# A hybrid attention and SwiGLU layer on one core: loads reordered at the start, partial output tiles begun early, one weight block of the down projection loaded later

## The chip, the cores and the metric

One core of one Trainium2 chip. The metric is device time in microseconds of one execution of the whole kernel; 665.92 us is the median of three runs before the change (665.73 to 667.33).

## What is computed

One decoder layer on x of 512 tokens by 1024 features, float32, then a final RMSNorm:

```
xn = rms_norm(h, norm1_g)
aq, ak, av, bq, kc, vc, ksl, vsl, kw, vw, gl = split_columns(xn @ w_in)
o_a = mixer_dilated(aq, ak, av)                    # 8 heads, three dilation patterns
o_b = g0 * o_cmp + g1 * o_slc + g2 * o_win         # 8 heads: compressed, selected, window
h = h + concat(o_a, o_b) @ w_out
hn = rms_norm(h, norm2_g)
h = h + (silu(hn @ w_gate) * (hn @ w_up)) @ w_down # hidden width 2816
out = rms_norm(h, norm_f_g)
```

The bias tables of attention come from a small table `rel_bias` by relative distance.

## The kernel before, in words

Every matrix product is made in three parts: an operand is split into a high part (a cast to float32r) and a low part (operand minus high), and TensorE adds high x high, high x low and low x high in one PSUM bank (`mm3`, lines 86 to 90). For a weight tile, `split` (line 77) loads it into one of three `w_raw` buffers on SP's queue (line 80), and writes high and low into one of five `w_hl` buffers, by ScalarE, VectorE or GpSimd as the table `ENG` says (lines 70, 72, 83).

**Order of work.** Most of the kernel is laid out as a program in order, and a planner (the tile framework) assigns each instruction its place on its engine from a timeline that it simulates, earlier program text first where several are ready; it also hands out the buffers. Where the source says `tc.manual_schedule(...)`, the named engines keep the order of the source. `tc.issue_after(x)` puts the instructions of its block behind x on x's engine alone. Each engine works in its own order and waits for what an instruction needs; SP's queue issues the transfers, one after the other, and waits in the same way.

**Start (lines 99 to 204).** SP issues `g_sb` (the norm gains, line 106), `rel_sb` and `oh_sb` (lines 144, 147), then x and the first weights. Twelve 128 x 128 products of ones (line 153) keep TensorE busy, four small products (line 157) build the bias rows. `load(kt)` (line 175) brings one of eight row blocks of x (line 177), scales and splits it on ScalarE and VectorE (lines 178, 179), and `project_0` makes the first projections. ScalarE loads its function table when its first function, the scaling of x, comes.

**Attention (lines 300 to 569).** Projections, bias tables, scores, softmax, transposes and the products with v, for 16 heads in the order of `PLAN`. `out_a` (line 481) makes half of the output projection for each of eight feature tiles and stores it, with x added, as `hp` in DRAM. The last head ends in `finish_head` and `finish_pair` (lines 360 to 371), which write the last of eight mixed tiles, high part on ScalarE (line 70), low part on GpSimd (line 371).

**Passage (lines 572 to 780).** The buffers of pool `ff` lie where those of attention were, so the first transfer into them waits for attention's last reader. `out_b(f)` (line 641) loads `hp` (line 643), makes the other half of the output projection over the mixed tiles 4 to 7 in one of four PSUM banks (two `proj`, two `S`), and VectorE adds (line 650). From it `lower` and `upper` (lines 614, 627) make the operands X1 and X2 of the feed-forward products, and `turn` (line 607) transposes the tile for the second norm. The products of gate and up are made by a scheme with seven products for eight (Strassen's, in Winograd's form), with sums of weights and of operands made on VectorE. `weights(j)` (line 691) is a generator that loads, adds and splits the weights of unit j in two parts; `first_part` and `second_part` (lines 718 to 747) are the unit's products.

```
    for f in range(KT - DELAY, KT):
        turn(f)
    w0.update(next(ahead))
    units = {0: first_part(0, w0)}
    with tc.issue_after(done):
        units[1] = first_part(1)
```

**Down projection (lines 785 to 1000).** Again seven products for eight, each over eleven row blocks in six steps (`PAIRS`). B11, B21, B22 and B12 are the four blocks of `w_down`, eleven loads of 256 KB each. SP keeps a written order (line 818): B11, B21, the residual `h1d` (line 832), B22, B12, then the final gain row `gf` (line 839). In a product's step, `prepare` splits both operands, and then the side work of that product runs: sums of operands on VectorE (`s1` to `s4`), weights added into B11 by accumulating transfers on GpSimd's queue (`add_w`, line 859), and `t3`, which adds B22 to B12 on VectorE. VectorE, ScalarE, GpSimd and TensorE keep the order of the source here. In the table, a product has its banks, its two operands, whether it starts the banks, its side work, what is evicted after it, and which output tiles are then closed. `close` squares a finished tile on ScalarE and multiplies its left half by `gf` on VectorE (`gain`), in the fourth step of the following product.

Of the kernel before, what the change touches and what calls it, by code (L numbers as in the profile page):

```python
# [11 lines left out]
F32 = mybir.dt.float32  # L12
F32R = mybir.dt.float32r
AF = mybir.ActivationFunctionType
ALU = mybir.AluOpType
# [36 lines left out]
def tile_hybrid_layer(ctx: ExitStack, tc: tile.TileContext, xT, w_qk0, w_t, w_av, w_vb, w_o, w_gu, w_d,  # L52
# [10 lines left out]
    def bank(tag):  # L63
        return psum.tile([P, 512], F32, name=tag, bufs=BANKS[tag])
# [9 lines left out]
    def tt(e, out, in0, in1, op):  # L74
        engines[e].tensor_tensor(out=out, in0=in0, in1=in1, op=op)  # L75

    def split(src, n, hi, lo):

        raw = ws.tile([P, WC], F32, name="w_raw", bufs=BUFS["w_raw"])
        nc.sync.dma_start(raw[:, :n], src)  # L80
        w = ws.tile([P, 2, WC], F32R, name="w_hl", bufs=BUFS["w_hl"])
        copy(hi, w[:, 0, :n], raw[:, :n])
        engines[lo].tensor_tensor(out=w[:, 1, :n], in0=raw[:, :n], in1=w[:, 0, :n].bitcast(F32), op=ALU.subtract)  # L83
        return w

    def mm3(ps, w, sl, xh, xl, first, last, skip=False):

        nc.tensor.matmul(ps, w[:, 0, sl], xh, start=first, stop=False, skip_group_check=skip)  # L88
        nc.tensor.matmul(ps, w[:, 0, sl], xl, start=False, stop=False, skip_group_check=skip)  # L89
        nc.tensor.matmul(ps, w[:, 1, sl], xh, start=False, stop=last, skip_group_check=skip)  # L90
# [12 lines left out]
    ii = const.tile([P, 64], F32, name="ii")  # L103
    nc.vector.tensor_tensor(out=ii, in0=ident[:, 0:64], in1=ident[:, 64:128], op=ALU.add)
    g_sb = const.tile([P, 2, KT], F32, name="g_sb")
    nc.sync.dma_start(g_sb, gT.rearrange("p (a k) -> p a k", a=2))
    cb_sb = const.tile([P, 2], F32, name="cb_sb")
    cw2_sb = const.tile([P, 3, DH], F32, name="cw2_sb")
    pos_sb = const.tile([P, 2, CSTRIDE], F32, name="pos_sb")
# [31 lines left out]


    rel_sb = const.tile([33, 16], F32, name="rel_sb")
    nc.sync.dma_start(rel_sb[0:32], rel)
    nc.vector.memset(rel_sb[32:33], 1.0)
    oh_sb = at.tile([33, 2, TW], F32, name="PTh")
    nc.sync.dma_start(oh_sb, oh.rearrange("b (a v) -> b a v", a=2))
    gd = dram.tile([16, RB, TW], F32, name="gd")
    gs = at.tile([16, 2, TW], F32, name="PTl")
    g1 = dram.tile([16, TW], F32, name="gh")  # L150
    warm = bank("S")
    for _ in range(12):
        nc.tensor.matmul(warm[:, :P], ones, ones, start=True, stop=True)
    for a in range(2):
        for c in range(2):
# [325 lines left out]
    def out_a(f, tok):  # L481

        w = split(w_o[f, :, 0:512], 512, *ENG[tok][:2])
        ps = bank("proj")
        for ft in range(4):
            mm3(ps, w, slice(ft * P, (ft + 1) * P), mixh[ft], mixl[ft], ft == 0, ft == 3)
        xr = at.tile([P, S], F32, name="pf", bufs=BUFS["pf"])
        nc.sync.dma_start(xr, xT[f * P:(f + 1) * P, :])
        if MISC["oa"] == "v":
            nc.vector.tensor_tensor(out=xr, in0=ps, in1=xr, op=ALU.add)  # L490
        else:
            y = at.tile([P, S], F32, name="pf", bufs=BUFS["pf"])
            nc.scalar.copy(y, ps)
            tt(MISC["oa"], xr, xr, y, ALU.add)
        nc.sync.dma_start(hp[f * P:(f + 1) * P, :], xr)
# [45 lines left out]
    for step in PLAN.split():  # L541
        n, i = step[0], step[1:]
        if n == "A":
            mix_a(int(i[0]), int(i[1]))
        elif n == "B":
            mix_b(int(i[0]), int(i[1]), i[2] == "w")
        elif n == "C":
            made["cmp", int(i)] = cmp_probs(made["b", int(i)], int(i), made["mlp"][0])
        elif n == "q":
            made["q", int(i)] = make_q(proj_t(2 * int(i) - 2, step), "Qa", e=MISC["tq"])  # L550
        elif n == "k":
            made["k", int(i)] = make_k(proj_t(2 * int(i) - 1, step), "a", 0, e=MISC["tk"])
        elif n == "b":
            made["b", int(i)] = make_q(proj_t(10 + int(i), step), "Qb", 2, MISC["tb"])
        elif n == "s":
            made["ksl"] = make_k(proj_t(8, step), "b", 1, 2, MISC["ts"])
        elif n == "w":
            made["kw"] = make_k(proj_t(9, step), "b", 2, 2, MISC["tw"])
        elif n == "v":
            project_vb((2 * int(i), 2 * int(i) + 1), step)  # L560
        elif n == "r":
            made["r" + i] = blocks(6 + int(i), int(i), step)
        elif n == "c":
            made["c" + i] = compress(made["r" + i], int(i), step)
        elif n == "m":
            made["mlp"] = compress_mlp((made["c0"], made["c1"]))
        elif n == "o":
            out_a(int(i), step)
    ph1.close()


# [8 lines left out]
    def split2(raw, hi, lo, w=None):  # L580

        if w is None:
            w = ff.tile([P, 2, 2, WC], F32R, name="hl2", bufs=BUFS["hl2"])
        copy(hi, w[:, 0], raw)
        tt(lo, w[:, 1], raw, w[:, 0].bitcast(F32), ALU.subtract)
        return w
# [40 lines left out]
    def upper(k, e):  # L627
# [10 lines left out]
        copy("a", X2[0][:, k, 2:5], f)  # L638
        tt("v", X2[1][:, k, 2:5], f, X2[0][:, k, 2:5].bitcast(F32), ALU.subtract)

    def out_b(f):
        xr = ff.tile([P, S], F32, name="g", bufs=BUFS["g"])
        nc.sync.dma_start(xr, hp[f * P:(f + 1) * P, :])
        w = split(w_o[f, :, 512:1024], 512, *ENG["ob"])
        ps = bank(("proj", "S")[f % 2])
        for ft in range(4, KT):
            mm3(ps, w, slice((ft - 4) * P, (ft - 3) * P), mixh[ft], mixl[ft], ft == 4, ft == KT - 1)
        h1 = ff.tile([P, S], F32, name="h1", bufs=BUFS["h1"])
        h1s[f] = h1
        nc.vector.tensor_tensor(out=h1, in0=ps, in1=xr, op=ALU.add)  # L650

    ss = ff.tile([P, NT, 2], F32, name="ss", bufs=1)

# [37 lines left out]
    def weights(j):  # L691

        l0 = raw2()
        nc.sync.dma_start(l0[:, 0], w_gu[j, 0, :, 0:WC])
        if j == 0:
            cd = raw2()
            c, d = cd[:, 0], cd[:, 1]
        else:
            c, d = raw1(), raw1()
        nc.sync.dma_start(c, w_gu[j, 1, :, 0:WC])  # L700
        nc.sync.dma_start(d, w_gu[j, 1, :, WC:])
        tt("v", l0[:, 1], c, d, ALU.add)
        w0 = split2(l0, "a", "v")
        yield {"a": w0[:, :, 0], "S1": w0[:, :, 1]}
        l1, l2 = raw2(), raw2()
        nc.sync.dma_start(l1[:, 1], w_gu[j, 0, :, WC:])
        tt("v", l1[:, 0], l0[:, 1], l0[:, 0], ALU.add)
        w1 = split2(l1, "a", "v")
        tt("v", l2[:, 0], l1[:, 0], l1[:, 1], ALU.add)
        tt("v", l2[:, 1], c, l0[:, 0], ALU.add)  # L710
        yield {"S2": w1[:, :, 0], "b": w1[:, :, 1], "S4": split1(l2[:, 0], "a", "v"), "S3": split1(l2[:, 1], "a", "v"),
               "d": split1(d, "a", "v")}

    def product(ps, w, X, b, first):
# [44 lines left out]
    for f in range(KT):  # L759
# [8 lines left out]
        if f == 2:  # L768
            ahead = weights(0)
            w0 = next(ahead)  # L770
    for f in range(KT - DELAY, KT):
        turn(f)
    w0.update(next(ahead))
    units = {0: first_part(0, w0)}
    with tc.issue_after(done):
        units[1] = first_part(1)
    second_norm()
# [45 lines left out]
    with tc.manual_schedule(engines={mybir.EngineType.SP}):  # L823
        r11 = [raw2() for _ in PAIRS]
        B11 = r11[:5] + [r11[5][:, 0:1]]
        load_w(B11, 0, 0)
        x0 = [ff.tile([P, n, WC], F32, name=tag, bufs=1)
              for n, tag in ((4, "X10"), (4, "X11"), (10, "X20"), (10, "X21"))]
        B21 = [x0[k // 2][:, 2 * (k % 2):2 * (k % 2) + 2] for k in range(4)] + [x0[2][:, 8:10], r11[5][:, 1:2]]
        load_w(B21, 1, 0)  # L830
        for t in range(NT):
            nc.sync.dma_start(x0[2][:, 2 * t:2 * t + 2], h1d[t].rearrange("p (c n) -> p c n", c=2))
        B22 = [x0[3][:, 2 * k:2 * k + 2] for k in range(5)] + [raw1()[:, None]]
        load_w(B22, 1, 1)
        B12 = [ws.tile([P, 2, WC], F32, name="w_hl", bufs=BUFS["w_hl"]) for _ in range(5)] + [raw1()[:, None]]
        load_w(B12, 0, 1)
        gf = [ff.tile([P, HD], F32, name="g", bufs=BUFS["g"]) for _ in range(2)]
        for c in range(2):
            nc.sync.dma_start(gf[c], gf_row[:, c * HD:(c + 1) * HD].to_broadcast([P, HD]))
# [22 lines left out]
    def t2(k):  # L862
        if k < 4:
            add_w(1, 1)(k)
        else:
            tt("v", B11[k], B11[k], B22[k], ALU.add)

    def t3(k):
        tt("v", B12[k], B12[k], B22[k], ALU.add)

    def evict(ps, th, c, sign=1):

# [21 lines left out]
    def store(t):  # L894
# [7 lines left out]
        (ps_a, A11, B11, True, (s3, add_w(0, 1)), [(ps_a, 0, 0)], []),  # L902
        (ps_b, A12, B21, True, (s1,), [(ps_b, 0, 0)], [(0, 0), (1, 0)]),
        (ps_c, A21, B11, True, (s2, t2), [(ps_c, 1, 1)], []),
        (ps_a, A21, B11, False, (s4, add_w(1, 0)), [(ps_a, 0, 1, -1)], []),
        (ps_c, A12, B22, False, (t3,), [(ps_c, 0, 1)], [(0, 1), (1, 1)]),
        (ps_a, A11, B12, False, (), [(ps_a, 1, 1, -1), (ps_a, 1, 0)], [(2, 1), (3, 1)]),
        (ps_b, A22, B11, True, (), [], [])]
    steps = [(n, k) for n in range(7) for k in range(len(PAIRS))]

# [152 lines left out]
```

## Time and profile before

| | |
|---|---|
| median of three runs | 665.92 us (665.73 to 667.33) |
| the profiled execution | 669.47 us, of which span 667.6 us |
| TensorE busy | 628.0 us, 94% of the span, 3876 products |
| VectorE busy | 530.5 us, 79% |
| ScalarE busy | 379.5 us, 57% |
| GpSimd busy | 170.0 us, 25% |
| DMA | 92.29 MB, mean 138 GB/s |

The profile is of one execution; its times run from the span's start. PE is TensorE, PEld its weight loads, DVE VectorE, ACT ScalarE, POOL GpSimd, SP SyncE; a q behind a name is that engine's queue of transfers and waits. A product's duration holds the time in the pipe, so products overlap; in the chain of work that ended last, a piece lasts from its start to the next one's. In a row of the timeline the brackets give how long the engine stood idle before the instruction and what ended that. Tile names carry no buffer numbers.

### The profile page before, as it was taken

How to read it: one execution, taken by the hardware profiler on the slowest of the kernel's cores; microseconds unless marked ns; L12 is line 12 of the kernel's file. 1: busy time of each engine (PE TensorE's matmuls, PEld its weight loads, DVE VectorE, ACT ScalarE, POOL GpSimd, SP SyncE). 2: the span in 40 equal slices, each digit the busy share in tenths (PEclk: the TensorE clock that was granted, in tenths of full speed). 3: DMA queues.
4: the chain of work that ended last, by engine and by line, in shares of the span. 5: the costliest groups of instructions: out<-in, count | busy, mean ns of one | idle time of the engine just before them, and what ended most of it. 6: DMA issues, size and time to landing. Idle time of an engine off the chain costs nothing.

```text
span 667.6 us, 11272 instructions
## 1 busy us (share of the span) xinstructions
PE 628.0 (94%) x3876; PEld 560.3 (84%) x3876; DVE 530.5 (79%) x1072; ACT 379.5 (57%) x785; POOL 170.0 (25%) x214
## 2 busy tenths in 40 slices
PE   9999997989999999987899999999999999859995
PEld 6878887868878888767799999999999988748784
DVE  4558867567787768649899989989999779669995
ACT  4553566245684668747864555555555636615572
POOL 6635852063445555430000000000000040414000
PEclk9999999979999999989899999999999999969998
DMA  5766576346415651043543333233233499949011
GB/s 178 211 189 188 168 182 165 100 132 164 130 36 172 187 192 33 1 163 106 189 141 102 108 127 122 87 111 109 97 113 108 164 258 322 305 85 160 1 63 63
DMA packets 52803, 92.29 MB, mean 138 GB/s; under 512 B 7643, under 2 KB 10971, under 8 KB 52748
## 3 DMA queue, kind: packets, MB, share of 16 engines
q1 hardware_dynamic: 47852, 82.68, 39.3%
q0 software_dynamic: 4320, 7.87, 6.8%
q10 hardware_dynamic: 576, 1.05, 0.4%
q8 instruction: 30, 0.49, 0.3%
q14 instruction: 25, 0.20, 0.1%
HBM read 76.32 MB, written 7.64 MB: 126 GB/s over the span
## 4 chain that ended last, share of the span: by engine, by line
PE 70%; DMA 11%; DVE 9%; ACT 5%; issue 3%; SPq 1%; POOL 1%; ACTq 0%; DVEq 0%; POOLq 0%
PE proj L88 8%; PE proj L90 8%; PE proj L89 8%; PE S L88 6%; PE S L89 6%; PE S L90 6%; PE PT L339 3%; DMA g<-in_gf_dram 2%; DMA X<-h1d 2%; PE S L316 2%; PE O L355 2%; PE O L358 2%; PE S L317 2%; DMA w_raw<-in_w_t_dram 1%; DMA X<-in_w_d_dram 1%
## 5 line engine op out<-in xcount | busy, mean ns | idle before, releaser
L859 POOL DMA_DIRECT2D raw<-in_w_d_dram x30 | 26.5, 1041 | 287.8 <-DVE hl L75 280.8
L70 ACT CAST hl<-raw 128x1024 fp32r<-128x1024 f32 (+1 forms) x69 | 70.5, 1022 | 40.5 <-PE S L930 16.7
L75 DVE TENSOR_TENSOR hl<-raw,hl 128x1024 fp32r<-128x1024 f32 (+1 forms) x69 | 81.2, 1178 | 3.0 <-ACT hl L70 2.9
L70 ACT CAST w_hl<-w_raw 128x512 fp32r<-128x512 f32 (+2 forms) x76 | 43.3, 576 | 63.6 <-PE S L90 19.2
L83 POOL TENSOR_TENSOR w_hl<-w_raw,w_hl 128x512 fp32r<-128x512 f32 (+1 forms) x47 | 61.2, 1306 | 65.2 <-ACT w_hl L70 26.2
L336 POOL TENSOR_SCALAR P<-P,den 128x512 f32<-128x512 f32 (+1 forms) x96 | 51.1, 551 | 39.9 <-DVE den L328 28.1
L324 ACT ACTIVATE P<-P,mn 128x512 f32<-128x512 f32 (+1 forms) x96 | 53.5, 558 | 11.8 <-DVE mn L322 11.5
L75 DVE TENSOR_TENSOR PTl<-PT,PTh 128x512 fp32r<-128x512 f32 (+2 forms) x96 | 43.8, 482 | 10.2 <-ACT PTh L349 9.7
L349 ACT CAST PTh<-PT 128x512 fp32r<-128x512 f32 (+2 forms) x96 | 38.1, 426 | 22.7 <-PE PT L339 18.8
L88 PE MATMUL S<-X,w_hl 128*128 128x256 f32 x176 | 49.9, 284 | 1.0 <-DVE h1t L75 0.5
L88 PE MATMUL S<-X,hl 128*128 128x256 f32 x176 | 50.0, 284 | 0.7 <-ACT xf L724 0.7
L322 DVE CUSTOM_DVE_ANT_0 P<-S,T 128x512 f32<-128x512 f32 (+1 forms) x96 | 43.9, 483 | 8.2 <-PE S L317 6.7
L89 PE MATMUL S<-X,hl 128*128 128x256 f32 x176 | 50.0, 284 | 0.3 <-DVE X L75 0.3
L89 PE MATMUL S<-X,w_hl 128*128 128x256 f32 x176 | 49.8, 283 | 0.0
L90 PE MATMUL S<-X,hl 128*128 128x256 f32 x176 | 49.7, 282 | 0.0
L90 PE MATMUL S<-X,w_hl 128*128 128x256 f32 x176 | 49.6, 283 | 0.0
L88 PE MATMUL proj<-xh,w_hl 128*128 128x512 f32 x112 | 46.1, 412 | 1.2 <-DVE va L281 1.1
L70 ACT CAST w_hl<-raw 128x512 fp32r<-128x512 f32 x45 | 27.3, 620 | 32.3 <-PE S L90 25.7
L90 PE MATMUL proj<-xh,w_hl 128*128 128x512 f32 x112 | 45.6, 407 | 0.0
L89 PE MATMUL proj<-xl,w_hl 128*128 128x512 f32 x112 | 45.4, 406 | 0.0
L83 DVE TENSOR_TENSOR w_hl<-w_raw,w_hl 128x512 fp32r<-128x512 f32 (+1 forms) x37 | 26.1, 710 | 15.0 <-ACT w_hl L70 14.9
L339 PE MATMUL PT<-ident,P 128*128 128x128 f32 x240 | 36.1, 273 | 0.8 <-POOL P L336 0.8
(305 smaller groups left out, 2047.5 us busy)
## 6 DMA issues: line engine op xcount, KB each, us to landing
raw<-in_w_gu_dram SPq DMA_DIRECT2D x46, 256.0 KB, 3.3
w_raw<-in_w_gu_dram SPq DMA_DIRECT2D x42, 256.0 KB, 2.7
raw<-in_w_d_dram POOLq DMA_DIRECT2D x30, 256.0 KB, 8.1
w_raw<-in_w_t_dram SPq DMA_DIRECT2D x28, 256.0 KB, 3.1
X<-in_w_d_dram SPq DMA_DIRECT2D x20, 256.0 KB, 7.5
T<-gd SPq DMA_DIRECT2D x64, 64.0 KB, 2.0
w_raw<-in_w_o_dram SPq DMA_DIRECT2D x16, 256.0 KB, 3.0
raw<-in_w_d_dram SPq DMA_DIRECT2D x12, 256.0 KB, 3.8
```

Of the source, the lines that this page charges most:

```text
L70: nc.scalar.copy(out, in_)
L75: engines[e].tensor_tensor(out=out, in0=in0, in1=in1, op=op)
L83: engines[lo].tensor_tensor(out=w[:, 1, :n], in0=raw[:, :n], in1=w[:, 0, :n].bitcast(F32), op=ALU.subtract)
L88: nc.tensor.matmul(ps, w[:, 0, sl], xh, start=first, stop=False, skip_group_check=skip)
L89: nc.tensor.matmul(ps, w[:, 0, sl], xl, start=False, stop=False, skip_group_check=skip)
L90: nc.tensor.matmul(ps, w[:, 1, sl], xh, start=False, stop=last, skip_group_check=skip)
L322: nc.vector.tensor_tensor_reduce(out=pp, in0=sv, in1=T[:, S - w:], op0=ALU.add, op1=ALU.min, scale=1.0, scalar=3e38, accum_out=mn[:, t:t + 1])
L324: nc.scalar.activation(pp, pp, AF.Exp, bias=mn[:, t:t + 1], scale=-1.0, accum_out=den[:, t:t + 1])
L336: nc.gpsimd.tensor_scalar(pp, pp, den[:, t:t + 1], 1.0, op0=ALU.mult, op1=ALU.mult)
L339: nc.tensor.transpose(pv[:, kb * P:(kb + 1) * P], pp[:, kb * P:(kb + 1) * P], ident)
L349: nc.scalar.copy(ov[0], pv)
L859: nc.gpsimd.dma_start(B11[k][:, i], rows_w(kh, ch, k, i), accum_op=ALU.add)
```

## The change

Start: x is the first transfer on SP; `g_sb`, `rel_sb` and `oh_sb` go to ScalarE's queue, ScalarE runs one small Square before, and nine products of ones take the place of twelve. Passage: `out_b` is cut in two; `out_b_start` makes the nine products over the mixed tiles 4 to 6, for tiles 0 to 3 ahead of the rest, and for tile 4, in a `PT` bank, behind the last TensorE instruction of the last head. The first products of unit 0 come before the last three turns, and `weights` yields its second part in two. Down projection: B12 has no buffers of its own; `load_12` loads it on GpSimd's queue into B21's, in the fourth product, `t3` and the sixth product use it there, and the accumulation `add_w(1, 0)` moves from the fourth to the fifth product.

```diff
-    nc.sync.dma_start(g_sb, gT.rearrange("p (a k) -> p a k", a=2))
+    nc.scalar.dma_start(g_sb, gT.rearrange("p (a k) -> p a k", a=2))
...
-    nc.sync.dma_start(rel_sb[0:32], rel)
+    nc.scalar.dma_start(rel_sb[0:32], rel)
...
-    nc.sync.dma_start(oh_sb, oh.rearrange("b (a v) -> b a v", a=2))
+    nc.scalar.dma_start(oh_sb, oh.rearrange("b (a v) -> b a v", a=2))
...
+    nc.scalar.activation(nt[:, 0:1], ones[:, 0:1], AF.Square)
     warm = bank("S")
-    for _ in range(12):
+    for _ in range(9):
...
+    head_end = [i for i in nc.cur_bb.bb.instructions[-60:] if i.engine == mybir.EngineType.PE][-1]
     ph1.close()
...
+    started = {}
+
+    def out_b_start(f):
+
+        w = split(w_o[f, :, 512:1024], 512, *ENG["ob"])
+        ps = bank("PT" if f == 4 else ("proj", "S")[f % 2])
+        for ft in range(4, KT - 1):
+            mm3(ps, w, slice((ft - 4) * P, (ft - 3) * P), mixh[ft], mixl[ft], ft == 4, False)
+        started[f] = w, ps
+
     def out_b(f):
+        if f not in started:
+            out_b_start(f)
+        w, ps = started.pop(f)
         xr = ff.tile([P, S], F32, name="g", bufs=BUFS["g"])
         nc.sync.dma_start(xr, hp[f * P:(f + 1) * P, :])
-        w = split(w_o[f, :, 512:1024], 512, *ENG["ob"])
-        ps = bank(("proj", "S")[f % 2])
-        for ft in range(4, KT):
-            mm3(ps, w, slice((ft - 4) * P, (ft - 3) * P), mixh[ft], mixl[ft], ft == 4, ft == KT - 1)
+        ft = KT - 1
+        mm3(ps, w, slice((ft - 4) * P, (ft - 3) * P), mixh[ft], mixl[ft], False, True)
...
+    for f in range(4):
+        out_b_start(f)
+    with tc.issue_after(head_end):
+        out_b_start(4)
...
         w1 = split2(l1, "a", "v")
+        yield {"S2": w1[:, :, 0], "b": w1[:, :, 1]}
         tt("v", l2[:, 0], l1[:, 0], l1[:, 1], ALU.add)
         tt("v", l2[:, 1], c, l0[:, 0], ALU.add)
-        yield {"S2": w1[:, :, 0], "b": w1[:, :, 1], "S4": split1(l2[:, 0], "a", "v"), "S3": split1(l2[:, 1], "a", "v"),
+        yield {"S4": split1(l2[:, 0], "a", "v"), "S3": split1(l2[:, 1], "a", "v"),
                "d": split1(d, "a", "v")}
...
-    for f in range(KT - DELAY, KT):
-        turn(f)
+    units = {0: first_part(0, w0)}
+    early = [i for i in nc.cur_bb.bb.instructions[-40:] if i.engine == mybir.EngineType.PE][-1]
+    with tc.issue_after(early):
+        for f in range(KT - DELAY, KT):
+            turn(f)
     w0.update(next(ahead))
-    units = {0: first_part(0, w0)}
+    w0.update(next(ahead))
...
-        B12 = [ws.tile([P, 2, WC], F32, name="w_hl", bufs=BUFS["w_hl"]) for _ in range(5)] + [raw1()[:, None]]
-        load_w(B12, 0, 1)
...
+    def load_12(k):
+        for i in range(B21[k].shape[1]):
+            nc.gpsimd.dma_start(B21[k][:, i], rows_w(0, 1, k, i))
+
     def t3(k):
-        tt("v", B12[k], B12[k], B22[k], ALU.add)
+        tt("v", B21[k], B21[k], B22[k], ALU.add)
...
-        (ps_a, A21, B11, False, (s4, add_w(1, 0)), [(ps_a, 0, 1, -1)], []),
-        (ps_c, A12, B22, False, (t3,), [(ps_c, 0, 1)], [(0, 1), (1, 1)]),
-        (ps_a, A11, B12, False, (), [(ps_a, 1, 1, -1), (ps_a, 1, 0)], [(2, 1), (3, 1)]),
+        (ps_a, A21, B11, False, (s4, load_12), [(ps_a, 0, 1, -1)], []),
+        (ps_c, A12, B22, False, (t3, add_w(1, 0)), [(ps_c, 0, 1)], [(0, 1), (1, 1)]),
+        (ps_a, A11, B21, False, (), [(ps_a, 1, 1, -1), (ps_a, 1, 0)], [(2, 1), (3, 1)]),
```

## Rows read from the trace of the kernel before

**Rows 1.** Stretches of 20 us: busy us (instructions) by engine, clock, DMA, GB/s.
```profile
core 0: us, PE busy (x) PEld busy (x) DVE busy (x) ACT busy (x) POOL busy (x), PEclk, DMA share, GB/s
300.00:320.00 20.00, 15.03 (x89) 13.06 (x87) 20.00 (x38) 16.07 (x33) 0.00 (x0) 0.91 0.41 151
...
580.00:600.00 20.00, 9.96 (x33) 7.66 (x33) 10.80 (x16) 4.61 (x7) 1.92 (x3) 0.74 0.52 117
600.00:620.00 20.00, 20.00 (x90) 16.57 (x89) 19.76 (x26) 11.43 (x17) 7.91 (x9) 1.00 0.85 142
```

**Rows 2.** Waits of PE and of DVE, 535 to 600: us in total, times, longest.
```profile
PE S L929 <- DVE hl L75: 10.0, 1, 10.0
...
DVE X L75 <- DMA g<-in_gf_dram: 10.5, 1, 10.5
```

**Rows 3.** Timeline of SP's queue, 505 to 660: start, us, issue.
```profile
566.51 6.43 SPq L813 DMA_DIRECT2D w_hl<-in_w_d_dram  x10
...
573.94 1.20 SPq L839 DMA_DIRECT2D g<-in_gf_dram  x2
```

**Rows 4.** Chain that ended last, 530 to 667: start, us, what.
```profile
573.94 14.81 DMA g<-in_gf_dram
...
593.08 0.43 PE S L930
...
597.35 0.43 PE S L928
...
598.04 0.23 PE S L930
...
629.47 0.50 PE PT L929
```

**Rows 5.** Stretch of 3 us inside DVE's wait, columns as in rows 1.
```profile
585.00:588.00 3.00, 0.00 (x0) 0.00 (x0) 0.00 (x0) 0.00 (x0) 0.00 (x0) 0.92 1.12 261
```

**Rows 6.** Timeline of DVE: end of its wait, first `t3`, one split.
```profile
589.20 1.29 DVE L75 TENSOR_TENSOR X<-X,g 128x512 f32<-128x512 f32 x2 [10.48 <-DMA g<-in_gf_dram]
...
612.11 1.22 DVE L75 TENSOR_TENSOR w_hl<-w_hl,X 128x1024 f32<-128x1024 f32 x1
...
628.20 1.21 DVE L75 TENSOR_TENSOR hl<-w_hl,hl 128x1024 fp32r<-128x1024 f32 x1
```

**Rows 7.** Timeline of POOL's queue: two pairs of accumulating loads, third product.
```profile
574.91 1.76 POOL L859 DMA_DIRECT2D raw<-in_w_d_dram  x2 [0.73 <-DVE hl L75]
578.42 1.75 POOL L859 DMA_DIRECT2D raw<-in_w_d_dram  x2 [1.74 <-DVE hl L75]
```

**Rows 8.** Timeline of the start, all engines.
```profile
0.74 0.38 SPq L106 DMA_DIRECT2D g_sb<-in_gT_dram  x1
...
1.06 5.49 PE L153 MATMUL S<-ones 128*128 128x128 f32 x24 [1.06 <-DVE ones L102]
...
2.09 0.36 SPq L177 DMA_DIRECT2D Qb<-in_xT_dram  x1
...
5.20 1.28 ACT L178 ACT_TABLE_LOAD   x1 [5.20 <-DMA Qb<-in_xT_dram]
...
8.09 0.73 PE L88 MATMUL PT<-xh,w_hl 128*128 128x512 f32 x2
```

**Rows 9.** Timeline of PE behind the first projections.
```profile
45.68 0.50 PE L88 MATMUL proj<-xh,w_hl 128*128 128x512 f32 x1 [1.11 <-DVE va L281]
```

**Rows 10.** Timeline of the passage, 277 to 345.
```profile
289.34 0.50 PE L88 MATMUL proj<-act,w_hl 128*128 128x512 f32 x1 [2.04 <-ACT act L70]
...
290.67 1.30 SPq L643 DMA_DIRECT2D g<-hp  x3
...
293.36 0.69 DVE L650 TENSOR_TENSOR h<-proj,g 128x512 f32<-128x512 f32 x1 [2.51 <-DMA g<-hp]
...
314.74 1.09 PE L611 MATMUL PT<-ident,h 128*128 128x128 f32 x4 [3.49 <-DVE h L650]
```

**Rows 11.** Waits of DVE, 285 to 345: us in total, times, longest.
```profile
DVE h L650 <- DMA g<-hp: 3.7, 2, 2.5
...
DVE X L75 <- ACT X L70: 2.0, 2, 1.7
```

## The prediction

> **What bounds the kernel now.** I read the busy time in stretches of 20 us first, then the waits inside the poor stretches, then the queues behind those waits. Beside the start, two stretches are poorest in TensorE (PE): the passage from attention to the feed-forward part (300 to 320 us, 15.03 of 20 busy) and the down projection at 580 to 600, with 9.96 of 20, the largest single hole [rows 1]. There VectorE (DVE) waits 10.5 us for the final gain row gf, once, and PE 10.0 us for DVE [rows 2]. The multiplication by gf (`gain`, called from `close` in the third product) stands in DVE's hand-written order, so everything behind it on DVE stands too. gf is late because of the queue in front of it: SP spends 566.51 to 573.94 on the eleven loads of B12 (ten into w_hl, one into w_raw) and only then issues gf, which lands 14.81 us later [rows 3, 4], with the DMA engines full to the last (share 1.12 in 585 to 588) [rows 5].
>
> What PE loses at 580 to 600 is more than the wait: the granted clock is 0.74 there, and in the chain eleven products (593.08 to 597.35) take 0.43 instead of 0.23 us each, 1.2 instead of 2.4 GHz, 2.2 us in all [rows 1, 4]. But this is not what sets the end. From 589.20 DVE works with hardly a pause (19.76 of 20 us in 600 to 620) [rows 1, 6], and PE is still held by it at 629.47: that product starts as the split begun at 628.20 ends [rows 4, 6]. So up to about 629 the down projection goes as fast as DVE goes, and a gain there is DVE's gain, not PE's.
>
> **The sum, part by part.** It is made against the profiled execution, 669.47 us (span 667.6 and 1.9 around it); that is 3.55 us above the median of 665.92.
>
> Late weights B12. Eleven loads of 256 KB (2.88 MB) leave SP's queue ahead of gf. By issue, gf moves from 573.94 to about 566.5; by bytes, 2.88 MB at the 261 GB/s of that stretch are 11 us, so instead of 588.75 it lands by 577.7 at the worst [rows 4, 5]. DVE needs it at 578.7 (589.20 less 10.5) [rows 6, 2]. The wait should vanish: 10.5 us. The low end is 9 (gf some late, or a small wait next), the high end 12.2 (PE's 10.0 and its 2.2 of slow clock both back). I take 10.5, because DVE is the engine that holds PE at 629. What is late next is DVE's own work, which is full.
>
> Where B12 goes. The loads now go into B21's tiles, on POOL's queue, behind the eight accumulating loads of the third product. POOL is free at 580.2 and takes 0.88 us for one issue (1.75 for two) [rows 7], so it issues all eleven by 589.8, and the accumulations moved to the fifth product start from there. The first reader, `t3(0)`, stands at 612.11 and would come at 601.6 [rows 6]; the first two loads are issued by 581.9 and, even if they take gf's 14.81, land by 596.7 [rows 4]: 4.9 us to spare, and more for each later one, since a product of 66 x 0.23 = 15 us takes six of these steps. The accumulations feed the last product, a whole product after that. Cost 0, and the cover is this slack.
>
> What speaks against it is that DVE is full all the while and POOL must write the descriptors. The rows show no such price: two issues took 1.76 us while DVE worked (574.91) and 1.75 while it stood still (578.42) [rows 7]. The Trainium skill, SBUF — State Buffer (SBUF: two separate sides), says that a VectorE instruction in a two-port mode locks GpSimd out, that a DMA issued from GpSimd then waits for its descriptors, and advises SP or ACT for it. By that rule the loads could come late, and the rival below gives its price in rows; by these rows the sum stands.
>
> Start. SP issues g_sb, rel and oh before x; x goes out at 2.09 instead of 0.74, so 1.35 us come off [rows 8]. The table load (5.20, 1.28 us) begins only when x has landed [rows 8]; the early Square puts it under x's flight. ACT now issues three transfers (some 0.4 each, as on SP) and loads the table by about 3.3, before x lands at 3.85: covered by 0.5 us; without that cover, ACT's part of the gain shrinks. Upper end 2.63. Nine warm-up products instead of twelve end at about 5.0 (24 records took 5.49) [rows 8], which only frees PE for what comes 2 us sooner; should the first 13 products run at the lower level, 0.2 us each [rows 4] gives the 2.6 back, so the lower end is 0. PE also waits 1.11 us at 45.68 for va, behind loads [rows 9], which keeps part of any early start. I take 1.8: the 1.35, along which SP's whole order moves, and a third of the 1.28.
>
> Fifth output tile. Its nine products (9 x 0.23 = 2.05 us) go into the 2.04 us that PE stands before 289.34, while ACT, DVE and POOL finish the last head [rows 10]. PE is not last there. The residual transfers go out only at 290.67, when attention's last reader has ended, and DVE's first sum starts at 293.36, waiting for them [rows 10]; DVE is then full (20.00 of 20 us in 300 to 320) [rows 1], and PE's longest stop, 3.49 us at 314.74, is for DVE. So I cost it at 0 by itself.
>
> Order of the first unit's weights, its first products before the last three turns. DVE's work is the same; four splits and three sums can only be moved behind the sums on which PE waits. What can come back is DVE's own idle time in 285 to 345: of 3.7 us for the residual the 1.2 after the first, and 2.0 for a cast on ACT [rows 11], 3.2 in all. Upper end 4.5 (with a later product of DVE's no longer awaited), lower end -1 (turns or splits now late for the second norm). I take 1.5, about half of the 3.2.
>
> The planner orders attention anew from a simulated timeline, with a start that has moved: 0, and 2 either way for the range.
>
> Sum: 10.5 + 1.8 + 1.5 = 13.8 us; 669.47 becomes 655.7, and the median 665.92 becomes **652.1**.
>
> **The rivals.** A: only the late weights count; the start is given back at 45.68 and DVE keeps the passage as long as it is. 665.92 - 10.5 = 655.4. For it: PE's waits at 45.68 and 314.74 are both for other work. Against: SP's whole order moves up.
> B: the passage gives back what PE lost in it. PE works 15.03 of 20 us in 300 to 320 [rows 1]; with the 4.5 of the upper end and the whole 2.6 of the start: 665.92 - 10.5 - 4.5 - 2.6 = 648.3. Against: DVE at 20.00.
> C, slower than before: the eleven loads on POOL's queue become the new wait. `t3` stands on DVE, and behind it the splits of the fifth and sixth products, so each microsecond that a load is late beyond its slack is one of the end. The last `t3` would come some 15 us after the first, at 616.6; to eat that and the 13.8 us, the last load must land at 630.4, so with gf's landing an issue must take (630.4 - 580.2 - 14.8) / 11 = 3.2 us instead of 0.88. At 3.6 us the time is some 670. The equal rows at 574.91 and 578.42 are against it. What the Trainium skill, SBUF — State Buffer (SBUF: two separate sides), describes would be such a price.
> D: the new order of attention costs one more stretch like 300 to 320, 5.0 us of PE [rows 1]: 657.1.
> That gf stays late (the change does not do what it says) would need the accumulations alone to hold it past 578.7; it lies with D in time, at most.
>
> **How the numbers follow.** Forecast 0.56 (650 to 654.5), A 0.17, B 0.14, D with gf still partly late 0.09, C 0.04. The likeliest is 652.1. The range 646 to 658.5 takes in A, B and D with 2 us for the new order; C and the far ends stay out. Under about 0.3%, 2 us, a measurement of this kernel can't tell a change from none. Faster 0.92, same 0.04 (D at its worst), slower 0.04 (C).
>
> **What would show it.** DVE's wait for gf gone from the list of waits and PE at the upper clock level through 580 to 600: the largest term. DVE still without pause up to the sixth product: that its gain, not PE's, counts. No wait of DVE at `t3`: C falls. x issued first, the first product at about 5.5 to 6.3 instead of 8.09, and PE's end of the first projection 1 to 2.6 us earlier: the start. Nine products of the fifth tile before the last head's tile is ready, with DVE's first sum no earlier against POOL's last subtraction: that this tile is worth little. The prediction is wrong if gf still lands after DVE wants it, if `t3` waits, or if attention takes over 3 us more or less than before.

## The result, and the profile after

The change ran in **658.65 us** (median of four runs, 656.49 to 661.05) beside 666.62 us for the kernel before on the same chip (four runs, 665.73 to 669.58): a ratio of **0.9874, 95% interval [0.9824, 0.9923]**, or 8.4 us with 5.1 to 11.7. Faster, as forecast, but by 8.4 us where 13.8 were forecast. 658.65 lies just above the upper end of the range, 658.5; counted from the 665.92 for which the range was given, the ratio makes it 657.5, just inside. The profiled execution took 657.67 us (span 655.9), 11.8 us less than that of before; of the two, that of before lies 2.85 us above its median here and that of after 0.98 below. So the profiles tell where the time went, and the ratio how much it was.

Some moments of the two profiled executions, read from the start of the instruction named (us from the start of the span):

| | before | after | after is ahead by |
|---|---|---|---|
| first product of the first projections | 8.1 | 4.9 | 3.2 |
| last product of the first projections | 43.8 | 42.8 | 1.0 |
| last product of the last head | 286.9 | 287.7 | -0.8 |
| first Silu of the feed-forward part | 341.5 | 341.4 | 0.1 |
| first product of the down projection | 535.9 | 535.1 | 0.8 |
| last product of the down projection | 659.1 | 647.4 | 11.7 |

So 10.9 of the 11.7 us of span come from the down projection. The start brings 3.2, keeps 1.0 at the end of the first projections, and attention turns that into a loss of 0.8. These are two executions; how far attention differs from one execution to the next is told with e9 to e12.

Stretches of 20 us of the kernel after (the columns are those of [rows 1]):

```profile
core 0: us, PE busy (x) PEld busy (x) DVE busy (x) ACT busy (x) POOL busy (x), PEclk, DMA share, GB/s
...
180.00:200.00 20.00, 16.65 (x102) 14.06 (x101) 17.00 (x53) 15.09 (x43) 9.82 (x16) 1.00 0.16 55
...
300.00:320.00 20.00, 12.71 (x79) 10.38 (x77) 20.00 (x40) 16.86 (x36) 0.00 (x0) 0.93 0.53 195
...
580.00:600.00 20.00, 19.24 (x85) 15.38 (x84) 20.00 (x29) 10.26 (x14) 15.09 (x21) 1.00 1.02 251
600.00:620.00 20.00, 19.32 (x84) 15.16 (x83) 20.00 (x24) 11.71 (x16) 0.00 (x0) 1.00 0.37 67
```

Against [rows 1], PE has 19.24 us of work in 580 to 600 instead of 9.96, at the upper clock level; DVE is at 20.00 of 20 in both stretches, and PE's missing 0.7 in each is DVE's doing. The passage is no fuller: 12.71 instead of 15.03.

The waits of DVE and of PE from 545 to 660, after:

```profile
DVE hl L75 <- ACT hl L70: 2.3, 7, 0.7
DVE X L982 <- PE proj L954: 1.8, 1, 1.8
DVE X L75 <- ACT g L674: 0.8, 1, 0.8
...
PE PT L953 <- DVE hl L75: 0.8, 1, 0.8
PE S L953 <- DVE hl L75: 0.6, 1, 0.6
```

The wait for gf [rows 2] is gone, and nothing of its size stands in its place: neither engine waits for a load. The queues tell the same. SP's:

```profile
564.88 0.33 SPq L835 DMA_DIRECT2D w_raw<-in_w_d_dram  x1
565.60 1.02 SPq L859 DMA_DIRECT2D g<-in_gf_dram  x2
```

gf is issued at 565.60 instead of 573.94 [rows 3]. POOL's queue, with the eleven loads on line 890 between two groups of accumulating loads (line 879):

```profile
577.66 1.76 POOL L879 DMA_DIRECT2D raw<-in_w_d_dram  x2 [1.75 <-DVE hl L75]
578.73 3.92 POOL L890 DMA_DIRECT2D X<-in_w_d_dram  x6
583.16 0.54 POOL L890 DMA_DIRECT2D X<-in_w_d_dram  x1 [0.51 <-DMA raw<-in_w_d_dram]
...
587.89 0.54 POOL L890 DMA_DIRECT2D raw<-in_w_d_dram  x1
588.54 5.35 POOL L879 DMA_DIRECT2D raw<-in_w_d_dram  x6
```

All are out by 588.4. And DVE's multiplication by gf and its first `t3`:

```profile
577.88 1.29 DVE L75 TENSOR_TENSOR X<-X,g 128x512 f32<-128x512 f32 x2
...
600.45 1.23 DVE L75 TENSOR_TENSOR X<-X,X 128x1024 f32<-128x1024 f32 x1
```

Neither row has a wait in brackets. They stand 11.32 and 11.66 us earlier than in [rows 6]; 0.76 of that came from before the down projection, so the wait itself gave 10.6, and the way from there to the first `t3` 0.3 more.

### The profile page after: what moved, and what is told of

Its sections match the earlier page's. It is cut to its first block, busy times and chain, and to the rows that moved or that the text cites. A ratio compares the mean times of both kernels' runs of the same rounds, so it can differ in the third digit from the quotient of the medians.

```text
span 655.9 us, 11277 instructions
## 1 busy us (share of the span) xinstructions
PE 623.6 (95%) x3870; PEld 555.2 (85%) x3870; DVE 533.6 (81%) x1072; ACT 378.5 (58%) x786; POOL 176.9 (27%) x225
## 4 chain that ended last, share of the span: by engine, by line
PE 66%; DVE 15%; DMA 5%; ACT 5%; issue 4%; POOL 2%; SPq 1%; ACTq 0%; DVEq 0%; POOLq 0%
PE proj L89 8%; PE proj L88 8%; PE proj L90 8%; PE S L88 6%; PE S L89 6%; PE S L90 6%; DVE hl L75 3%; PE PT L340 3%; PE S L317 2%; PE O L356 2%; PE S L318 2%; DMA w_raw<-in_w_t_dram 2%; PE O L359 1%; PE PT L88 1%; PE PT L89 1%
## 5 line engine op out<-in xcount | busy, mean ns | idle before, releaser
L75 DVE TENSOR_TENSOR hl<-raw,hl 128x1024 fp32r<-128x1024 f32 (+1 forms) x70 | 82.1, 1175 | 3.8 <-ACT hl L70 3.8
L75 DVE TENSOR_TENSOR PTl<-PT,PTh 128x512 fp32r<-128x512 f32 (+2 forms) x96 | 44.3, 484 | 8.7 <-ACT PTh L350 8.1
```

## The experiments

All ratios are against the kernel before on the same chip. e1 to e4, e5 to e8 and e9 to e12 each share one set of runs of before, on three chips (medians 668.45, 667.50 and 670.13 us), so ratios, not times, are compared across the sets.

| run | what it is | median us | ratio, 95% interval |
|---|---|---|---|
| e1 | late weights alone | 658.87 | 0.9849 [0.9811, 0.9887] |
| e2 | only gf's loads ahead of B12's | 656.73 | 0.9816 [0.9780, 0.9852] |
| e3 | start alone | 670.26 | 1.0034 [1.0005, 1.0063] |
| e4 | passage alone | 667.05 | 0.9975 [0.9948, 1.0003] |
| e5 | the change again | 658.40 | 0.9864 [0.9826, 0.9902] |
| e6 | gf first + passage | 656.76 | 0.9836 [0.9805, 0.9868] |
| e7 | the change without its start | 656.52 | 0.9828 [0.9797, 0.9859] |
| e8 | the change, POOL's two groups swapped | 667.52 | 0.9994 [0.9971, 1.0017] |
| e9 | e7 + the three transfers on ScalarE's queue | 656.85 | 0.9813 [0.9786, 0.9839] |
| e10 | e7 + early Square, nine warm-up products | 661.24 | 0.9869 [0.9841, 0.9898] |
| e11 | e6 + the three transfers | 658.00 | 0.9827 [0.9798, 0.9856] |
| e12 | e7 without the fifth output tile | 657.53 | 0.9828 [0.9799, 0.9858] |

### e1 and e2: is it the wait for gf, and does it need the moved loads?

e1 makes only the down projection's part of the change:

```diff
-        load_w(B12, 0, 1)
...
-        (ps_a, A21, B11, False, (s4, add_w(1, 0)), [(ps_a, 0, 1, -1)], []),
-        (ps_c, A12, B22, False, (t3,), [(ps_c, 0, 1)], [(0, 1), (1, 1)]),
+        (ps_a, A21, B11, False, (s4, load_12), [(ps_a, 0, 1, -1)], []),
+        (ps_c, A12, B22, False, (t3, add_w(1, 0)), [(ps_c, 0, 1)], [(0, 1), (1, 1)]),
```

> The kernel before with the down projection's part alone: B12 into B21's tiles on GpSimd's queue. My theory: the gain row's wait (10.5 us) goes and nothing takes its place, so about 10.5 us less than before (9 to 11.5). Rival: the down projection's part needs the early start or the passage beside it, or TensorE's 2.2 us of lower clock come back too: under 8, or over 12 us less.

e2 leaves B12 where it was and only turns two neighbours on SP's queue:

```diff
-        B12 = [ws.tile([P, 2, WC], F32, name="w_hl", bufs=BUFS["w_hl"]) for _ in range(5)] + [raw1()[:, None]]
-        load_w(B12, 0, 1)
         gf = [ff.tile([P, HD], F32, name="g", bufs=BUFS["g"]) for _ in range(2)]
         for c in range(2):
             nc.sync.dma_start(gf[c], gf_row[:, c * HD:(c + 1) * HD].to_broadcast([P, HD]))
+        B12 = [ws.tile([P, 2, WC], F32, name="w_hl", bufs=BUFS["w_hl"]) for _ in range(5)] + [raw1()[:, None]]
+        load_w(B12, 0, 1)
```

> The kernel before with one edit: the two loads of the gain row are issued ahead of B12 on SP's queue; B12 keeps its buffers and its queue. My theory: the wait is one of order on the queue, so this alone gives about 10 us, as much as the whole late loading (9 to 11.5 less than before). Rival: the bytes of B12 themselves crowd the DMA engines, so that the next thing (accumulated weights, B22) comes late in its place: 3 to 7 us less than before, with a new wait of VectorE or ScalarE for a transfer.

Measured: 10.1 us faster (7.6 to 12.6) and 12.3 us (9.9 to 14.7). In e2 SP's queue reads

```profile
567.56 1.02 SPq L837 DMA_DIRECT2D g<-in_gf_dram  x2
568.87 6.38 SPq L813 DMA_DIRECT2D w_hl<-in_w_d_dram  x10
```

and the stretch that was poorest is as full as in the change:

```profile
580.00:600.00 20.00, 19.25 (x84) 15.39 (x83) 20.00 (x29) 10.79 (x15) 9.21 (x12) 1.00 1.08 217
600.00:620.00 20.00, 19.34 (x84) 15.17 (x83) 20.00 (x26) 11.46 (x17) 1.54 (x2) 1.00 0.34 59
```

The down projection, from its first product to its last, takes 112.3 us in e1 and in e2, against 123.2 before and 112.3 after. So the term is 10.9 in both. It varies with the execution: e3 and e4 below have the down projection of before, with a wait for gf of 9.5 and 9.7 us and 122.2 us in all, and against these the term is 9.9. What made gf late was its place in the queue: the eleven loads may stay on SP if they stand behind gf. The place cost twice, in the issue (573.94 against 567.56) and in the flight, from issue to landing (DMA issues from 560 to 590, before and e2 in turn):

```profile
g<-in_gf_dram SPq DMA_DIRECT2D x2, 256.0 KB, 15.7
```

```profile
g<-in_gf_dram SPq DMA_DIRECT2D x2, 256.0 KB, 5.3
```

### e3 and e4: the start alone, the passage alone

e3:

```diff
-    nc.sync.dma_start(g_sb, gT.rearrange("p (a k) -> p a k", a=2))
+    nc.scalar.dma_start(g_sb, gT.rearrange("p (a k) -> p a k", a=2))
...
-    nc.sync.dma_start(rel_sb[0:32], rel)
+    nc.scalar.dma_start(rel_sb[0:32], rel)
...
-    nc.sync.dma_start(oh_sb, oh.rearrange("b (a v) -> b a v", a=2))
+    nc.scalar.dma_start(oh_sb, oh.rearrange("b (a v) -> b a v", a=2))
...
+    nc.scalar.activation(nt[:, 0:1], ones[:, 0:1], AF.Square)
     warm = bank("S")
-    for _ in range(12):
+    for _ in range(9):
```

> The kernel before with the start's part alone. Theory after seeing the changed kernel: the first product comes 3 us earlier, the first projection ends 1 us earlier, and the last head ends within 1 us of before: time within 1.5 us of before. Rival, as predicted: 1.8 us less, the lead of the start kept to the end of attention.

e4 is `out_b_start`, the generator's additional `yield`, and the first unit's products ahead of the last turns:

```diff
+    with tc.issue_after(head_end):
+        out_b_start(4)
...
+        yield {"S2": w1[:, :, 0], "b": w1[:, :, 1]}
...
+    units = {0: first_part(0, w0)}
+    with tc.issue_after(early):
+        for f in range(KT - DELAY, KT):
+            turn(f)
```

> The kernel before with the passage's part alone (fifth tile early, first products ahead of the last turns, weights in three parts). My theory: 1.5 us less than before, from VectorE's idle time (0 to 3). Rival: TensorE's whole loss there comes back, 4 us or more less; other rival: no gain, because VectorE has the same work.

Measured: the start alone is **slower**, by 2.3 us (0.3 to 4.2), which neither expectation had. The passage alone is 1.7 us faster with an interval that takes in zero (-0.2 to 3.5). The parts add up: 10.1 - 2.3 + 1.7 = 9.5, beside 9.1 for the change measured again (e5) and 8.4 at first. Nothing shows a part that works only together with another.

### e5 to e8: the change again, without its start, and with POOL's queue the other way round

e5 has no edit.

> The whole change once more, beside the others. Parts measured alone: -9.6 (late weights), +1.8 (start), -1.4 (passage). Theory: they add up, so about 9.2 us less than before (7.5 to 11). Rival: they work together and give the forecast 13.8 less.

e6 is e2's edit with e4's.

> The gain row ahead of B12 on SP's queue and the passage's part, with the start of before and B12 in its own buffers. Theory: the two add up, 11.7 and 1.4, so about 13 us less than before and the best so far (11 to 14.5). Rival: the late loading frees something that this lacks, so that it is no better than the whole change.

e7 is the change with the lines of e3 taken back.

> The whole change without the start's part. Theory: the start costs 1 to 2 us, since its lead is used up at 105 to 200 us by the other order of attention; so about 11 us less than before, 1 to 2 less than the whole change. Rival: the start gives its 1.8, so this is 1.8 more than the whole change.

e8 keeps the whole change and puts the eleven loads behind the accumulating loads on POOL's queue, instead of ahead of them:

```diff
-        (ps_a, A21, B11, False, (s4, load_12), [(ps_a, 0, 1, -1)], []),
-        (ps_c, A12, B22, False, (t3, add_w(1, 0)), [(ps_c, 0, 1)], [(0, 1), (1, 1)]),
+        (ps_a, A21, B11, False, (s4, add_w(1, 0)), [(ps_a, 0, 1, -1)], []),
+        (ps_c, A12, B22, False, (t3,), [(ps_c, 0, 1)], [(0, 1), (1, 1)]),
...
+            if (n, k) == (4, 0):
+                for q in range(len(PAIRS)):
+                    load_12(q)
```

> The whole change with GpSimd's queue in the other order: the accumulations into B11 stay in the fourth product, and the loads of B12 come behind them, from about 602 us instead of 580. The first t3 stands at about 601. Theory of the rival C (each microsecond that a load is late on VectorE is one of the end): VectorE waits for the transfer at t3 and the time is longer than the whole change by that wait, 4 to 12 us. Against it: the loads land 3 us after their issue and outrun t3, so that the wait is 3 us or less; or TensorE has slack there and the wait costs less than its length.

Measured: e7 is the faster one, 11.5 us against e5's 9.1 beside the same runs of before. Their intervals overlap, but the difference, some 2 us, is the one that e3 gives: the change is better off without its start. e6 lies with e7 (10.9), a little under what was expected of it.

e8 gives nearly the whole gain back: 0.4 us faster (-1.1 to 1.9). Its POOL queue, DVE's row and DVE's wait:

```profile
598.37 2.65 POOL L879 DMA_DIRECT2D raw<-in_w_d_dram  x3 [0.58 <-DVE hl L75]
600.45 3.29 POOL L890 DMA_DIRECT2D X<-in_w_d_dram  x5
604.46 0.54 POOL L890 DMA_DIRECT2D X<-in_w_d_dram  x1 [0.71 <-DMA raw<-in_w_d_dram]
...
610.09 0.54 POOL L890 DMA_DIRECT2D raw<-in_w_d_dram  x1
```

```profile
600.47 1.22 DVE L75 TENSOR_TENSOR hl<-X,hl 128x1024 fp32r<-128x1024 f32 x1
609.22 1.23 DVE L75 TENSOR_TENSOR X<-X,X 128x1024 f32<-128x1024 f32 x1 [7.53 <-DMA X<-in_w_d_dram]
```

```profile
DVE X L75 <- DMA X<-in_w_d_dram: 7.5, 1, 7.5
...
PE S L953 <- DVE hl L75: 6.6, 1, 6.6
```

The accumulating loads hold POOL until about 600.5 because each pair waits for a split on DVE (`<-DVE hl L75`), and the loads behind them are wanted at 601.7 (609.22 less 7.53). This is rival C of the prediction, built: one late load at the first `t3`, 7.53 us of DVE, 6.6 of PE. In the change the same eleven loads are issued from 578.73, some 22 us before that reader, and nothing waits. The down projection takes 120.3 us, 8.0 more than with the change, so nearly each microsecond of that wait is one of the end. What separates +0 from +9 us is the order of two groups on one queue.

### e9 to e12: what in the start costs, and what the fifth tile is worth

Laid side by side with the order of PE's products in e7's trace (3,876 rows), the trace of e9, which moves the three transfers alone, differs in 50 lines, all within the first 105 rows; that of e10, which has the Square and the nine products, differs in 394, spread over attention as far as row 1,729. The planner orders attention from a simulated timeline, and by these orders e10's two edits move that timeline where the transfers hardly do. So the start was cut there.

e9:

```diff
-    nc.sync.dma_start(g_sb, gT.rearrange("p (a k) -> p a k", a=2))
+    nc.scalar.dma_start(g_sb, gT.rearrange("p (a k) -> p a k", a=2))
...
-    nc.sync.dma_start(rel_sb[0:32], rel)
+    nc.scalar.dma_start(rel_sb[0:32], rel)
...
-    nc.sync.dma_start(oh_sb, oh.rearrange("b (a v) -> b a v", a=2))
+    nc.scalar.dma_start(oh_sb, oh.rearrange("b (a v) -> b a v", a=2))
```

> The change with its start cut to the three transfers on ScalarE's queue, so that x goes out first; the Square and the nine warm-up products are left out. Attention's written order then stays that of the kernel before but for the first few products. Theory (what costs the change its start is attention's other order, not the transfers): first product about 5 to 6.5 us instead of 7.9, PE's loss at 180 to 200 us near the 3.9 us of the kernel with both other parts (not 5.6), and 655 to 656.5 us, ratio about 0.982, at least as fast as that kernel's 656.5. Rival (moving x first is the cost, by what it pushes on ScalarE): about 658.4, ratio 0.9865, as the whole change.

e10:

```diff
+    nc.scalar.activation(nt[:, 0:1], ones[:, 0:1], AF.Square)
     warm = bank("S")
-    for _ in range(12):
+    for _ in range(9):
```

> The other half of the start alone: the early Square and nine warm-up products instead of twelve, the three transfers staying on SP's queue, with both other parts of the change. The start is then no more than about 1.3 us earlier on the chip, but attention's written order is another one. Theory (the other order is what loses): PE's loss at 180 to 200 us near 5.6 us, and 658 to 659 us, ratio about 0.986, some 2 us slower than with both other parts alone. Rival (the order costs nothing): 655.5 to 656.5, ratio 0.982.

e11 is e6 with the lines of e9.

> A candidate for the fastest: gf's two loads issued ahead of B12's on SP's queue, the passage part, and the three transfers on ScalarE's queue. If the transfers give their earlier start without attention's other order: 655 to 656 us, ratio about 0.981. If they give nothing: 656.7, ratio 0.9835, as with the first two alone.

Measured: 0.9813 for e9, 0.9869 for e10, 0.9827 for e11. Against e7 and e6, the three transfers alone are 1.0 and 0.6 us to the good, both well within the intervals. The stretch from 180 to 200 us shows the two orders best, since the clock is whole there in every kernel. Before, e9 and e10 in turn:

```profile
180.00:200.00 20.00, 18.86 (x116) 15.84 (x114) 17.86 (x60) 16.67 (x48) 9.86 (x16) 1.00 0.21 63
```

```profile
180.00:200.00 20.00, 18.88 (x115) 15.78 (x114) 17.87 (x59) 17.05 (x48) 9.87 (x16) 1.00 0.19 54
```

```profile
180.00:200.00 20.00, 16.65 (x106) 14.22 (x105) 16.98 (x54) 15.52 (x45) 9.83 (x16) 1.00 0.19 54
```

PE's busy time there falls into two groups with nothing between: 18.86 to 18.92 us in the nine kernels without the Square and the nine products (before, e1, e2, e4, e6, e7, e9, e11, e12), 16.62 to 16.65 in the five with both (after, e3, e5, e8, e10). That is 2.2 us. The waits of PE from 176 to 202 in the kernel after name what is in it:

```profile
PE O L356 <- ACT PTh L350: 1.5, 1, 1.5
PE PT L474 <- POOL cy L470: 1.3, 1, 1.3
```

Before and e9 have neither row there; e10 has both, with the same numbers. What is lost there doesn't come back later: from the last product of the first projections to the last product of the last head, the nine take 242.6 us in the mean (240.7 to 244.8), the five 245.0 (244.5 to 246.2). Two of the nine, e4 and e9, reach into the five, so one pair of profiles wouldn't show it. (The expectations of e9 and e10 put PE's loss from 180 to 200 at 3.9 and 5.6 us; by busy time it is 1.1 and 3.4, with a difference of 2.2 instead of 1.7.)

The times sort in the same way: of the kernels in which gf is early and nothing else waits, the seven with the old order have ratios of 0.9813 to 0.9849, the three with the other order (after, e5, e10) 0.9864 to 0.9874.

e10 pays a second price, so its time alone would not carry this. Its PE idles 1.16 us before the first product, and the granted clock falls behind it:

```profile
7.20 0.80 PE L88 MATMUL PT<-xh,w_hl 128*128 128x512 f32 x2 [1.16 <-ACT w_hl L70]
```

```profile
5.00:10.00 5.00, 3.84 (x11) 1.17 (x9) 2.98 (x5) 4.18 (x8) 1.34 (x2) 0.77 0.77 222
10.00:15.00 5.00, 5.00 (x11) 2.73 (x11) 2.95 (x5) 3.09 (x7) 4.57 (x4) 0.50 0.69 205
```

Its first projections end at 47.5 instead of e7's 43.6. That the gap made the clock fall is not shown: e7 and e4 idle 1.18 and 1.44 us at the same place and stay at 1.00. The change itself has no such gap (x comes earlier there) and no such fall, and is slower than e7 all the same; that comparison, e3's and the 180 to 200 rows carry the verdict.

e12 takes the fifth output tile out of e7, so that `out_b` is the old one:

```diff
-    for f in range(4):
-        out_b_start(f)
-    with tc.issue_after(head_end):
-        out_b_start(4)
```

> Late weights and the order of the first unit's weights, without the fifth output tile. Prediction's step (the tile is worth 0 by itself): the same time as with the tile, about 656.5 us, ratio 0.983, with PE's loss at 260 to 290 us about 7.4 instead of 5.5 and so much less at 290 to 345. Rival (the tile is what the passage part gains): about 658, ratio 0.985, as with the late weights alone.

Measured: 0.9828 with and without it. The tile does what it is meant to: from 260 to 290 PE is busy 28.32 us in e7, 26.08 in e12; the first Silu comes at 338.9 and 339.0. What it fills is a hole that nobody waited for. (The edit takes the early starts of tiles 0 to 3 out as well, but their nine products each stand ahead of the last head's end in both traces.)

## Why the prediction was right, and where it was too large

**Late weights: right, mechanism and size.** 10.5 was taken because DVE, not PE, holds the stage to 629. Measured 10.9, the same with either edit, and 9.9 against e3 and e4. gf had more room than thought: it landed 5.3 us after its issue from 565.60 on, by 572, where 577.7 was reckoned at the worst. The other reading, PE's wait and its slow clock both back (12.2), falls: PE is held to 19.24 and 19.32 of 20 by a full DVE, as the prediction said of 580 to 629.

**The loads on POOL: right, with more room than thought.** The cost of 0 rested on 0.88 us an issue and 4.9 us to spare; a plain load alone took 0.54 us. With stops between them the eleven took as long as reckoned, 9.7 us (578.73 to 588.43), but they landed some 7 us after their issue instead of 14.8 (issues from 560 to 605, after), the first about 586, 14 us ahead of the first `t3`:

```profile
X<-in_w_d_dram POOLq DMA_DIRECT2D x10, 256.0 KB, 7.3
```

The Trainium skill, SBUF — State Buffer (SBUF: two separate sides), lets VectorE's two-port modes lock GpSimd out while it writes descriptors. If DVE's sums and splits count as such, these loads should have been slow, with DVE busy 20.00 of 20 us. The trace shows no such price: a plain load alone took 0.54 us with DVE at work (583.16, after) and 0.54 while DVE stood still (604.46, e8). No run tells whether DVE's work here counts. Rival C's wait is real, but its cause is the queue's order, and e8 shows it at 7.5 us where the rival asked for slow issues.

**Start: the failed step.** It was 1.8 us to the good and is about 2 to the bad. x did go out first, and the table load lies under its flight:

```profile
0.73 0.41 ACTq L106 DMA_DIRECT2D g_sb<-in_gT_dram  x1
...
0.74 0.39 SPq L178 DMA_DIRECT2D Qb<-in_xT_dram  x1
...
2.31 1.28 ACT L151 ACT_TABLE_LOAD   x1 [2.31 <-issue]
...
4.91 1.20 PE L88 MATMUL PT<-xh,w_hl 128*128 128x512 f32 x2
...
6.04 1.57 PE L158 MATMUL proj<-PTh,rel_sb 33*16 33x320 f32 x4
```

The first product comes at 4.91 against 8.09 [rows 8], earlier than the 5.5 to 6.3 expected. But the four bias products that stood ahead of it now stand behind its first pair, and the lead is 1.0 at 43 us. (At the next product it is 2.0, 43.65 against the 45.68 of [rows 9], but e7, with the old start, has that product at 44.61, so half of this is from execution to execution.) The second half of the step was booked elsewhere, as "0, and 2 either way" for the planner's new order. In that order PE loses 2.2 us more from 180 to 200, and attention as a whole takes 2.4 more, short of the 3 us that the prediction named as a sign of being wrong. That eats the 1.0 and leaves 1.4 to the bad; that the whole is about 2 lies within the intervals. So the step that failed is the one that carries the start's lead through attention to the end and prices the new order at 0. The two terms together were +1.8 and are some -2, which is 3.8 of the 4.3 to 5.4 us between the forecast of 13.8 and the 8.4 to 9.5 measured.

**Fifth tile: right at 0.** After, the nine products stand ahead of the last head's tile, PE has no wait at 290.13 where it had 2.04 [rows 10], and DVE's first sum still comes 2.72 us after the residual transfers are issued (2.69 before):

```profile
287.92 0.40 PE L88 MATMUL PT<-act,w_hl 128*128 128x512 f32 x1
...
290.13 0.50 PE L88 MATMUL proj<-act,w_hl 128*128 128x512 f32 x1
```

```profile
291.47 1.29 SPq L658 DMA_DIRECT2D g<-hp  x3
```

```profile
294.19 0.69 DVE L663 TENSOR_TENSOR h<-proj,g 128x512 f32<-128x512 f32 x1 [2.54 <-DMA g<-hp]
```

**Order of the first unit's weights: size fits, not settled.** 1.5 was booked; e4 gives 1.7, e7 against e1 1.4, but e6 against e2 1.3 the other way. In the profiles, from the last head's last product to the first of the down projection, it is nearer 1: 247.9 us in the mean of the nine kernels with the whole passage part (247.1 to 249.0), 248.8 in the four with none of it (248.1 to 249.6). Of the 3.2 us of DVE's idle time that were to come back, the waits of DVE from 285 to 345, after, show the cast on ACT gone and the second residual not:

```profile
DVE h L663 <- DMA g<-hp: 3.4, 2, 2.5
...
DVE X L75 <- ACT X L70: 0.3, 1, 0.3
```

2.0 became 0.3, and 3.7 only 3.4 [rows 11]. PE now waits elsewhere for the same full DVE (waits of PE from 285 to 345, after):

```profile
PE PT L89 <- DVE X L638: 3.2, 2, 2.1
PE proj L89 <- DVE X L75: 2.5, 1, 2.5
```

With 0.8 at line 613, PE's waits for DVE are 6.5 us here, where they were 5.8 before (3.5 of them at 314.74 [rows 10]).

**Rivals.** D comes nearest, in time (657.1) and in its mechanism, the new order of attention, though at 2.2 us and not at 5.0. A is right that the late weights are nearly all there is and that the start is given back, but not at 45.68: that wait is gone in the change, and the lead is lost behind it. B falls: nothing shows 4.5 us from the passage. C falls for this order of the queue.

**Best version.** Seven kernels lie between 0.9813 and 0.9849, with intervals that overlap, and no run tells them apart. All have a lower ratio than the change, by 1 to 4 us. e2 is among them with two statements exchanged. Whether the Square or the nine products bring the slower order stays open: no run has one of them alone.

## What to carry to other kernels

When a small load is late, look first at what stands ahead of it in its queue: here the exchange of two neighbours was worth as much as a rebuilt schedule. Where a planner orders the work, a small edit at the start can be an edit of everything behind it, so time it alone, and compare the written order before crediting or blaming the edit itself. A hole of an engine on which nobody waits can be filled at no gain.

## What the runs showed of the hardware

- **A plain load takes less of GpSimd than an accumulating one.** Of 256 KB each, a plain load alone took 0.54 us and six in a row 3.92 (line 890); a pair of accumulating ones took 1.76, and six 5.35, one wait for a landing included (line 879), in the same 20 us with DVE full.
- **A transfer behind others lands later after its own issue.** gf's two loads landed 5.3 us after their issue in e2 and in the change, and 14.8 and 15.7 us before, behind eleven loads of 256 KB with the DMA engines full [rows 5].
- **The stops between GpSimd's loads are the program's own.** In the trace, transfers on this queue signal on eight semaphores in turn, and each waits first on the one that it will use, so until the load eight ahead of it has landed: the load at 583.16 (after) waits for that of 577.66, which landed at 582.88. These stops show no limit of GpSimd.
- **The clock at the start differs between executions.** In e10 the granted clock was 0.50 in 10 to 15 us, the lower of the two levels (1.2 GHz), with PE busy all the while, and in e1 and e2 it was 0.82 to 0.84 from 5 to 15, behind stops of PE of 1.16, 1.02 and 1.08 us ahead of the first product. e7 and e4, with 1.18 and 1.44, kept 1.00, so the length of that stop alone doesn't decide it. The kernel after, without it, has 1.00 over its first 50 us.
